# A hybrid attention and scan layer: the input projection taken in pairs of column slabs by a seven-product scheme, transposed, and kept in DRAM until attention and scan read it

## The chip, the cores and the metric

One core of a Trainium2 chip runs the whole layer. The metric is device time in microseconds (us); three runs of the kernel before gave a median of 1931.54 (1930.09 to 1934.35). The engines are named as the profile names them: PE (TensorE, matmul), PEld (its weight loads), DVE (VectorE), ACT (ScalarE), POOL (GpSimd), SP (SyncE, which here only issues DMAs).

## The reference

A sequence of 1024 tokens of width 1024 passes one layer:

```python
h = rmsnorm(x, g_pre)
q, k, v, g_att, z, xbc, dt, merge = split(h @ w_in)   # 1024 -> 12320 columns
o = diff_attention(q, k, v, rel_bias, lam)            # 8 heads, two softmax maps of width 64 each
y_att = (rmsnorm(o) * (1 - lambda_init) * silu(g_att)) @ w_att
xs, B, C = split(silu(causal_conv4(xbc)))             # 2048 + 8*128 + 8*128 columns
y = ssd_scan(xs, softplus(dt + dt_bias), -exp(a_log), B, C) + xs * d_skip
y_ssm = group_rmsnorm(y * silu(z)) @ w_ssm            # 8 groups
mixed = sigmoid(gate_att) * y_att + sigmoid(gate_ssm) * y_ssm
out = x + rmsnorm(mixed @ w_out, g_post)
```

All is float32. The projection `h @ w_in` is the largest product. In columns of 128 ("slabs") it has 8 each for q, k, v, g, 16 for z, 16 for x, 8 each for B and C, 16 for the gates, and 32 columns for dt.

## The kernel before

**Precision.** A float32 operand is kept as two tiles, a high half h (ACT copies the operand to a shorter format) and a low half l (the operand less h). `split` (L96) makes both: ACT the copy (L98), DVE or, if it is named, POOL the subtraction (L99). A product is three matmuls, h by h, h by l, l by h (`mm3`, L144; the matmul is L150). A slab of 128 columns for all tokens is thus 8 blocks of depth x 3 matmuls x 2 halves of 512 tokens, 48 matmuls of 512 columns.

**The start.** x is loaded in eight tiles, normed, transposed on PE (`ptx`, L235) and kept as hTH and hTL (L237, L238) through the whole kernel.

**The projection** is taken where it is needed. `load_cols` (L129) loads a slab of weights in two pieces of 128x512 and splits them. `proj_T` (L153) gives 128 output columns by 512 tokens in PSUM, for q, k, B, C, x and the gates; `proj_N` (L165) gives 128 tokens by 256 columns, for v with g, and for z. What comes out in PSUM is used there: L269 to L277 make the halves of q and k, L288 to L292 those of v and the gate, `conv_silu` (L498) copies it to the tile u and runs the convolution of four taps in two halves of 512 (L513, L515), L536 and L537 turn z into silu(z) in the token-major tile sz.

**Attention.** `attention` (L253) works a head after another, each in eight query blocks, `attend` (L311): scores `s` on PE (L322, L323), bias and maximum on DVE (L328, L331), the exponentials `p` on ACT (L342), the difference of the two maps on DVE (L357), transposes `pta` and their halves ah, al (L360 to L363), the product with v (`po`, L366, L367). The outputs are normed per head, multiplied by the gate (L305), transposed and stored in o_d.

**Scan.** `ssm` (L529) has eight groups; in each, eight chunks of 128 tokens pass through `prepare` (transposes px, xe at L578, xdt at L579, v on POOL at L580, the decay matrix mt: a load on ACT's DMA queue, ACT at L586 and L587, DVE at L588) and `advance` (products pd, the state st on POOL at L604, outputs v and yo at L609 to L614). `finish` norms, transposes and stores y_d.

**The order.** The Tile scheduler lays the instructions of each engine in one fixed order, by the program's order, dependences and buffers; an engine doesn't pass an instruction that waits. Gates (`gates`, L388) are projected between the heads and stored in sig_d. After the eight heads `branch_att` (L399) does the product with w_att, then the scan with its projections, then the rest of the gates, and at last (L655) the products with w_ssm and w_out.

Of the kernel before, what the change touches and what calls it, by code (L numbers as in the profile page):

```python
# [17 lines left out]
P = 128  # L18
# [5 lines left out]
DK = 64  # L24
# [23 lines left out]
CI, CU, CM, CE = 0, 128, 256, 384  # L48
NCONST = CE + NEAR
# [25 lines left out]
def tile_hybrid_layer(ctx: ExitStack, tc: tile.TileContext, x, g_pre, w_in, lq1, lk1, lq2, lk2,  # L75
# [9 lines left out]
    wts = ctx.enter_context(tc.tile_pool(name="wts", bufs=2))  # L85
# [33 lines left out]
    hTH = const.tile([P, KT, S], F32R, tag="hTH", name="hTH")  # L119
    hTL = const.tile([P, KT, S], F32R, tag="hTL", name="hTL")  # L120
# [6 lines left out]
    near_d = dram.tile([HEADS, NEAR], F32, name="near_d")  # L127

    def load_cols(w, row0, col0, width, tag, name, off=0, wh=None, wl=None, eng=None):  # L129

        if wh is None:
            wh = wts.tile([P, KT, width], F32R, tag=tag + "h", name=name + "h")
            wl = wts.tile([P, KT, width], F32R, tag=tag + "l", name=name + "l")
        for c in range(0, width - off, P):
            n = min(P, width - off - c)
            cols = slice(off + c, off + c + n)
            for k0 in range(0, KT, 4):
                raw = wts.tile([P, 4, P], F32, tag="raw", bufs=3, name=f"{name}r{off + c}_{k0}")
                r0 = row0 + k0 * P
                nc.sync.dma_start(raw[:, :, 0:n], w[r0:r0 + 4 * P, col0 + c:col0 + c + n].rearrange("(k p) c -> p k c", p=P))  # L140
                split(wh[:, k0:k0 + 4, cols], wl[:, k0:k0 + 4, cols], raw[:, :, 0:n], eng)
        return wh, wl

    def mm3(ps, terms):  # L144

        n = 3 * len(terms)
        i = 0
        for (ah, al), (bh, bl) in terms:
            for a, b in ((ah, bh), (ah, bl), (al, bh)):
                nc.tensor.matmul(ps, a, b, start=(i == 0), stop=(i == n - 1))  # L150
                i += 1

    def proj_T(w, half, name, rhs=None):  # L153

        wh, wl = w
        ps = psp.tile([P, 512], F32, tag="pp", name=name)
        sl = slice(half * 512, half * 512 + 512)
        if rhs is None:
            rhs = [(hTH[:, k, sl], hTL[:, k, sl]) for k in range(KT)]
        else:  # L160
            rhs = [(h[:, sl], l[:, sl]) for h, l in rhs]
        mm3(ps, [((wh[:, k, :], wl[:, k, :]), rhs[k]) for k in range(KT)])
        return ps

    def proj_N(w, t, n, name):  # L165

        wh, wl = w
        ps = psp.tile([P, 512], F32, tag="pp", name=name)
        sl = slice(t * P, (t + 1) * P)
        mm3(ps[:, 0:n], [((hTH[:, k, sl], hTL[:, k, sl]), (wh[:, k, 0:n], wl[:, k, 0:n])) for k in range(KT)])  # L170
        return ps
# [27 lines left out]
    with tc.tile_pool(name="norm", bufs=2, reuse_waits="tile") as work:  # L199
        def load_x(half):  # L200
            tiles = []
            for t in range(half * 4, half * 4 + 4):
                xt = work.tile([P, D], F32, tag="xt", bufs=8, name=f"xt{t}")
                nc.sync.dma_start(xt, x[t * P:(t + 1) * P, :])
                tiles.append(xt)
            return tiles

# [6 lines left out]
        nc.vector.tensor_copy(gcol, pg[:, 0:KT + 1])  # L214
        for half in range(2):
# [10 lines left out]
            for k in range(KT):  # L226
                if k % 4 < 2:
                    pt = pst.tile([P, 512], F32, tag="t", name=f"ptx{half}_{k}")
                elif k % 2 == 0:
# [183 lines left out]
    with tc.tile_pool(name="attn", bufs=2, reuse_waits="tile") as work:  # L413
        for h in range(HEADS):
            attention(h)
            gates(h)
# [320 lines left out]
```

## Time and profile before

| | |
|---|---|
| median of 3 runs | 1931.54 us |
| the profiled execution's own time | 1931.15 us |
| its span | 1929.4 us |
| granted TensorE clock | 0.989 |
| PE busy | 1828.1 us (95%), 10249 matmuls |
| DVE busy | 1183.5 us (61%), 2782 instructions |
| ACT busy | 862.4 us (45%) |
| POOL busy | 136.3 us (7%), 154 instructions |
| DMA | 169.34 MB, mean 88 GB/s |
| matmuls with w_att | from 734.43 us to the first with z's weights at 821.53 us |
| first matmul with w_ssm | 1640.72 us |

How to read what follows. A busy time is the time that the profiler shows instructions on an engine. Matmuls overlap, so the length of one (0.39) isn't its price; the distance between the starts of two in a row is. In a line of groups, "xN | busy, mean ns | idle before, releaser" gives the count, the sum, the mean of one, and what ended the idle time ahead of them. In a timeline the first number is the start, the second the length, and the bracket at the end is the idle time before it and what ended it. In a windows line the columns are the stretch, its length, then busy time (and count) of PE, PEld, DVE, ACT and POOL, the granted clock, the DMA share and GB/s.

### The profile page before, as it was taken

Reading aid. Unit: us, or ns where it says so; the run is one execution under the profiler, and the core shown is the slowest. Engines: PE = TensorE matmul, PEld = TensorE weight load, DVE = VectorE, ACT = ScalarE, POOL = GpSimd, SP = SyncE. Lnnn points to the kernel's source line nnn. Section 1 sums busy time; section 2 is a strip of 40 time slices with the busy share of each in tenths; the row PEclk is TensorE's granted clock in tenths of the full one; section 3 lists DMA queues with packets and bytes.
Section 4 is the critical chain, followed back from the end, with each engine's and each line's share of the span. In section 5 each row is a group of like instructions: output and inputs, shape, how many; then the busy total and the mean of one; then the engine's idle time right before and its main releaser. Section 6 shows DMA issues by size and latency. Waiting matters only on the chain. (4 is left out here: it accounts for less than half of the span.)

```text
span 1929.4 us, 27946 instructions
## 1 busy us (share of the span) xinstructions
PE 1828.1 (95%) x10249; PEld 1564.5 (81%) x10249; DVE 1183.5 (61%) x2782; ACT 862.4 (45%) x2135; POOL 136.3 (7%) x154
## 2 busy tenths in 40 slices
PE   6999999999999999999899989998989999999998
PEld 4888889789888878888787878787878777877786
DVE  5576486766757553247576767676757676545433
ACT  6455364545636442125445444545444545332221
POOL 1000000000000010001010101010101022000000
PEclk9999999999999999999999999999999999999999
DMA  6121222222122135513222222222222225653532
GB/s 204 55 75 56 53 58 59 70 61 60 54 54 66 37 125 178 166 34 79 70 61 72 63 69 63 70 65 71 63 64 64 69 50 173 220 172 134 175 110 71
DMA packets 222279, 169.34 MB, mean 88 GB/s; under 512 B 12733, under 2 KB 187167, under 8 KB 222143
## 3 DMA queue, kind: packets, MB, share of 16 engines
q1 hardware_dynamic: 169390, 117.21, 20.7%
q10 hardware_dynamic: 52752, 50.36, 9.0%
q8 instruction: 81, 1.33, 0.3%
q14 instruction: 56, 0.45, 0.1%
HBM read 129.63 MB, written 31.08 MB: 83 GB/s over the span
## 5 line engine op out<-in xcount | busy, mean ns | idle before, releaser
L150 PE MATMUL pz<-wzh,hTL 128*128 128x256 f32 (+1 forms) x512 | 152.0, 297 | 0.0
L150 PE MATMUL pz<-wzh,hTH 128*128 128x256 f32 (+1 forms) x512 | 149.6, 292 | 0.3 <-DVE dtr L539 0.3
L150 PE MATMUL pz<-wzl,hTH 128*128 128x256 f32 (+1 forms) x512 | 148.0, 289 | 0.0
L150 PE MATMUL pv<-wvh,hTH 128*128 128x256 f32 x512 | 144.5, 282 | 0.7 <-DVE kl L277 0.4
L150 PE MATMUL pv<-wvl,hTH 128*128 128x256 f32 x512 | 144.8, 283 | 0.0
L150 PE MATMUL pv<-wvh,hTL 128*128 128x256 f32 x512 | 144.0, 281 | 0.0
L586 ACT ACTIVATE mt<-mt,acs 128x128 f32<-128x128 f32 x256 | 85.6, 391 | 112.9 <-DMA mt<-arow_d 112.9
L580 POOL TENSOR_TENSOR v<-xb,dsk 128x256 f32<-128x256 f32 x64 | 51.1, 808 | 683.6 <-ACT xb L572 613.6
L331 DVE TENSOR_REDUCE ng<-s 128x2 f32<-128x1024 f32 (+2 forms) x96 | 91.3, 952 | 12.4 <-PE s L323 11.9
L150 PEld LDWEIGHTS pv<-wvh,hTH 128*128 128x128 f32 x512 | 97.0, 190 | 2.3 <-PE pv L150 0.5
L150 PEld LDWEIGHTS pz<-wzh,hTH 128*128 128x128 f32 x512 | 97.7, 191 | 1.5 <-PE pz L150 0.5
L150 PEld LDWEIGHTS pz<-wzl,hTH 128*128 128x128 f32 x512 | 97.6, 191 | 0.5
L150 PEld LDWEIGHTS pz<-wzh,hTL 128*128 128x128 f32 x512 | 97.1, 190 | 0.7
L150 PEld LDWEIGHTS pv<-wvl,hTH 128*128 128x128 f32 x512 | 96.7, 189 | 0.3
L150 PEld LDWEIGHTS pv<-wvh,hTL 128*128 128x128 f32 x512 | 96.2, 188 | 0.0
L342 ACT ACTIVATE p<-s,ngm 128x512 f32<-128x512 f32 (+3 forms) x128 | 76.7, 610 | 34.9 <-DVE ngm L337 34.8
L513 DVE SCALAR_TENSOR_TENSOR xT<-ux,cw,xT 128x512 f32<-128x512 f32 x96 | 75.7, 789 | 20.2 <-ACT xT L511 18.8
L607 PE MATMUL pd<-xdt,mt 128*128 128x64 f32 x512 | 66.6, 273 | 11.0 <-DVE st L605 4.8
L607 PEld LDWEIGHTS pd<-xdt,mt 128*128 128x128 f32 x512 | 62.4, 191 | 16.4 <-ACT mt L586 9.0
L366 PE MATMUL po<-vv,ah 128*128 128x256 f32 x288 | 74.8, 289 | 0.0
L289 DVE TENSOR_TENSOR vv<-pv,vv 128x128 fp32r<-128x128 f32 x64 | 18.6, 291 | 87.8 <-ACT vv L288 87.6
L367 PE MATMUL po<-vv,al 128*128 128x256 f32 x288 | 71.8, 282 | 0.0
(869 smaller groups left out, 5423.0 us busy)
## 6 DMA issues: line engine op xcount, KB each, us to landing
mt<-arow_d ACTq DMA_DIRECT2D x64, 256.0 KB, 4.9
sig_d<-gt ACTq DMA_DIRECT2D x32, 256.0 KB, 2.1
y_d<-yT ACTq DMA_DIRECT2D x32, 256.0 KB, 2.1
yT_l<-y_d SPq DMA_DIRECT2D x32, 256.0 KB, 5.7
xt<-in_x SPq DMA_DIRECT2D x8, 512.0 KB, 5.8
kh<-kh ACTq DMA_DIRECT2D x32, 128.0 KB, 2.3
kl<-kl ACTq DMA_DIRECT2D x32, 128.0 KB, 2.3
o_d<-oT ACTq DMA_DIRECT2D x16, 256.0 KB, 2.0
```

Of the source, the lines that this page charges most:

```text
L150: nc.tensor.matmul(ps, a, b, start=(i == 0), stop=(i == n - 1))
L289: nc.vector.tensor_tensor(vv[:, t, DV:], ps[:, 0:DV], f32(vv[:, t, 0:DV]), op=ALU.subtract)
L331: nc.vector.tensor_reduce(ng, s[:, :, 0:width], axis=AX.X, op=ALU.max, negate=True)
L342: nc.scalar.activation(p[:, m, lo:lo + width], s[:, m, 0:width], AF.Exp, bias=neg[:, m:m + 1], accum_out=sums[:, i, m:m + 1])
L366: nc.tensor.matmul(po[:, 0:256], ah[:, k, :], vv[:, k, :], start=(k == 0), stop=False)
L367: nc.tensor.matmul(po[:, 0:256], al[:, k, :], vv[:, k, :], start=False, stop=(k == qb))
L513: nc.vector.scalar_tensor_tensor(out_h, u[:, j:j + 512], cw[:, j, ct:ct + 1], out_h, op0=ALU.mult, op1=ALU.add)
L580: nc.gpsimd.tensor_tensor(v4(v), v4(xb[:, 0:256]), b4(dsk[:, hs]), op=ALU.mult)
L586: nc.scalar.activation(mt[:, i, :], mt[:, i, :], AF.Relu, scale=-1.0, bias=acs[:, c, g * HG + i:g * HG + i + 1])
L607: nc.tensor.matmul(pd[:, 0, i * PH:(i + 1) * PH], mt[:, i, :], xdt[:, i * PH:(i + 1) * PH], start=True, stop=True)
```

## The change

hTH, hTL, `load_cols`, `proj_T` and `proj_N` go from the projection. In their place stands `pair` (L160 of the changed kernel): two slabs of w_in at a time, all tokens, all transposed. Weights of a pair are seen as a 2 x 2 matrix of blocks (two slabs by two halves of the depth), h as a 2 x 2 matrix (two halves of the depth by two halves of the tokens), and the four blocks of the result come of seven products of blocks, where the plain way takes eight (Strassen's scheme in the form of Winograd). Each is 4 blocks of depth x 3 matmuls, so a pair takes 84 matmuls of 512 columns; two slabs took 96.

The seven combinations of h are made once, at the start (L249 and on), with the halves bh and bl; they take the room of hTH and hTL and more. The combinations of weights are made in each pair: s1 (L175), s2 (L176), a21 (L179) and s2 again (L195) by additions on POOL; each of seven operands is split by `halves` (L142), ACT for the high, POOL for the low half. The sums of the products go over four additions on DVE from PSUM (L189, L198, L208, L211), three copies on ACT, and one addition on POOL (L205). Gates go through ACT's tanh. Four stores on SP put a pair's halves into the DRAM tiles `slabs`.

What read PSUM before now loads a slab: q and k twice, so that the two maps lie as they did (`doubled`), v, which PE transposes (`ptv`), g, and in the scan u of the convolution at full width of 1024 and z, which PE transposes in `advance`. q's and k's low halves, the gate, the convolution and silu(z) thus work from SBUF on widths of 1024. The gate is kept transposed and multiplied into the transposed output (oT, on DVE). dt has its own small product (`steps`).

For the room that this takes, buffers shrink: x's tiles 8 to 6; qs and near 2 to 1; xT, bT, cT and sz 2 to 1; mt 3 to 2; v 7 to 6. The stores of o_d and y_d move from ACT's DMA queue to SP's. The pairs of head h+1 are written behind head h, the gates' pairs behind every second head and behind the first five scan groups, the pairs of scan group g+1 behind group g; `branch_att` moves behind the scan.

```diff
+    def halves(src, name):
+        h = prod.tile([P, 4, P], F32R, tag="ph", bufs=4, name=name + "h")
+        l = prod.tile([P, 4, P], F32R, tag="pl", bufs=4, name=name + "l")
+        split(h, l, src, nc.gpsimd)
+        return h, l
+
+    def product(ps, a, b, first):
+
         i = 0
...
+        for k in range(4):
+            for u, v in ((a[0], bh), (a[0], bl), (a[1], bh)):
+                nc.tensor.matmul(ps, u[:, k, :], v[:, b, k, :], start=first and i == 0, stop=i == 11,
+                                 skip_group_check=not first)
                 i += 1
...
+    def pair(c0, c1, gate=False):
...
+        a11, a21 = raw_half(c0, 0, f"a11_{nm}"), raw_half(c1, 0, f"a21_{nm}")
+        a22, a12 = raw_half(c1, 1, f"a22_{nm}"), raw_half(c0, 1, f"a12_{nm}")
...
+        p11 = halves(a11, f"p11_{nm}")
+        nc.gpsimd.tensor_tensor(s1, a21, a22, op=ALU.add)
+        nc.gpsimd.tensor_tensor(s2, s1, a11, op=ALU.subtract)
+        ps2 = halves(s2, f"ps2_{nm}")
+        p12 = halves(a12, f"p12_{nm}")
+        nc.gpsimd.tensor_tensor(a21, a21, a11, op=ALU.subtract)
+        ps3 = halves(a21, f"ps3_{nm}")
...
+        product(u, p11, B11, True)
+        m1 = staged(f"m1_{nm}")
+        nc.scalar.activation(m1, u, AF.Copy)
+        product(xx, ps2, T2, True)
+        x6 = staged(f"x6_{nm}")
+        nc.vector.tensor_tensor(x6, xx, m1, op=ALU.add)
+        ps1 = halves(s1, f"ps1_{nm}")
+        product(u, p12, B21, False)
+        c11 = staged(f"c11_{nm}")
+        nc.scalar.activation(c11, u, AF.Tanh if gate else AF.Copy, scale=0.5 if gate else 1.0)
+        nc.sync.dma_start(d0[:, 0:512], c11)
+        nc.gpsimd.tensor_tensor(s2, a12, s2, op=ALU.subtract)
+        product(xx, ps3, T3, False)
+        u3 = staged(f"u3_{nm}")
+        nc.vector.tensor_tensor(u3, xx, m1, op=ALU.add)
+        p22 = halves(a22, f"p22_{nm}")
...
+        product(v, ps1, T1, True)
+        m5 = staged(f"m5_{nm}")
+        nc.scalar.activation(m5, v, AF.Copy)
+        ps4 = halves(s2, f"ps4_{nm}")
+        nc.gpsimd.tensor_tensor(u3, u3, m5, op=ALU.add)
+        store(u3, d1, 1)
+        product(xx, p22, T4, False)
+        nc.vector.tensor_tensor(m1, xx, m1, op=ALU.add)
+        store(m1, d1, 0)
+        product(v, ps4, B22, False)
+        nc.vector.tensor_tensor(x6, v, x6, op=ALU.add)
+        store(x6, d0, 1)
...
-                xt = work.tile([P, D], F32, tag="xt", bufs=8, name=f"xt{t}")
+                xt = work.tile([P, D], F32, tag="xt", bufs=6, name=f"xt{t}")
...
+        def put(i, k, src, eng):
+            nc.scalar.activation(bh[:, i, k, :], src, AF.Copy)
+            eng.tensor_tensor(bl[:, i, k, :], src, f32(bh[:, i, k, :]), op=ALU.subtract)
...
+                    put(T2, k, t2, nc.vector)
+                    put(T3, k, t3, nc.gpsimd)
+                    put(T1, k, t1, nc.gpsimd)
+                    nc.gpsimd.tensor_tensor(t2, b1f[:, 4 + k, :], t2, op=ALU.subtract)
+                    put(T4, k, t2, nc.vector)
+                    put(B22, k, b22, nc.gpsimd)
...
+            q = doubled(OQ + h * P, half)
+            nc.scalar.activation(qs[:, :, sl], q, AF.Copy, scale=DK ** -0.5)
+            nc.vector.scalar_tensor_tensor(qs[hi, :, sl], q[hi], DK ** -0.5, f32(qs[hi, :, sl]), op0=ALU.mult, op1=ALU.subtract)
+            k = doubled(OK + h * P, half)
+            split(kh[:, :, sl], kl[:, :, sl], k)
...
+    def conv_silu(col, ct, dst, name):
+
+        u = work.tile([P, CONV - 1 + S], F32, tag="u", name=f"u{name}")
+        nc.gpsimd.memset(u[:, 0:CONV - 1], 0.0)
+        nc.sync.dma_start(u[:, CONV - 1:], slabs[col])
+        nc.scalar.activation(dst, u[:, CONV - 1:], AF.Identity, scale=cw[:, CONV - 1, ct:ct + 1], bias=cb[:, ct:ct + 1])
+        for j in range(CONV - 1):
+            nc.vector.scalar_tensor_tensor(dst, u[:, j:j + S], cw[:, j, ct:ct + 1], dst, op0=ALU.mult, op1=ALU.add)
+        nc.scalar.activation(u[:, 0:S], dst, AF.Tanh)
+        nc.vector.scalar_tensor_tensor(dst, u[:, 0:S], 1.0, dst, op0=ALU.add, op1=ALU.mult)
...
-            mt = work.tile([P, HG, P], F32, tag="mt", bufs=3, name=f"mt{nm}")
+            mt = work.tile([P, HG, P], F32, tag="mt", name=f"mt{nm}")
...
         for g in range(SG):
             ssm(g)
+            if g + 1 < SG:
+                for cols in ssm_pairs(g + 1):
+                    pair(*cols)
+            if g < 5:
+                pair(*gate_pairs[3 + g], gate=True)
```

Where the instructions come to stand is shown at three places, before and after. The first is POOL among the heads of attention. Before, POOL has two splits there in the time of one head (wm2, wm3, wm4 are the gates' weights behind three heads in a row):

```order
L99 TENSOR_TENSOR wm2l<-wm2r_0_3020,wm2h 128x512
L99 TENSOR_TENSOR wm2l<-wm2r_4_3024,wm2h 128x512
L99 TENSOR_TENSOR wm3l<-wm3r_0_3947,wm3h 128x512
L99 TENSOR_TENSOR wm3l<-wm3r_4_3951,wm3h 128x512
L99 TENSOR_TENSOR wm4l<-wm4r_0_4874,wm4h 128x512
L99 TENSOR_TENSOR wm4l<-wm4r_4_4878,wm4h 128x512
```

After, it has the splits and additions of whole pairs; 256_1280 is the pair of q's slab at column 256 and k's at 1280, for the third head:

```order
L175 TENSOR_TENSOR s_256_1280_1992<-a_256_1280_1986,a_256_1280_1988 128x512
L176 TENSOR_TENSOR s_256_1280_1993<-s_256_1280_1992,a_256_1280_1984 128x512
L179 TENSOR_TENSOR a_256_1280_1986<-a_256_1280_1986,a_256_1280_1984 128x512
L100 TENSOR_TENSOR p_256_1280l<-a_256_1280_1984,p_256_1280h 128x512
L100 TENSOR_TENSOR ps_256_1280l<-s_256_1280_1993,ps_256_1280h 128x512
L205 TENSOR_TENSOR u_2176_3200_1416<-u_2176_3200_1416,m_2176_3200_1435 128x512
L195 TENSOR_TENSOR s_256_1280_1993<-a_256_1280_1990,s_256_1280_1993 128x512
L100 TENSOR_TENSOR p_256_1280l<-a_256_1280_1990,p_256_1280h 128x512
L100 TENSOR_TENSOR ps_256_1280l<-a_256_1280_1986,ps_256_1280h 128x512
L100 TENSOR_TENSOR ps_256_1280l<-s_256_1280_1992,ps_256_1280h 128x512
L100 TENSOR_TENSOR p_256_1280l<-a_256_1280_1988,p_256_1280h 128x512
```

The weights' low halves have moved from DVE to POOL, with the additions of the scheme behind and between them; in all POOL has 749 rows, where it had 159.

The second place is PE in the attention of the second head, at the fourth query block's scores. Before, what stands between the steps of attention is the gate's projection pg, with hTH and hTL as the weights' partners:

```order
L322 MATMUL s_3_0_1743<-kh_1231,qs_1230 128x512
L323 MATMUL s_3_0_1743<-kl_1232,qs_1230 128x512
L150 MATMUL pg_0_2101<-hTH,wm1h 128x512
L150 MATMUL pg_0_2101<-hTL,wm1h 128x512
L366 MATMUL po_1_1696<-vv_1233,ah_1_1688 128x256
L150 MATMUL pg_0_2101<-hTH,wm1l 128x512
L367 MATMUL po_1_1696<-vv_1233,al_1_1689 128x256
```

After, the products of the next head's pair stand there, pu and px being two of the pair's sums in PSUM, and p_256_1280l the low half that POOL makes:

```order
L383 MATMUL s_3_0_1622<-kh_1472,qs_1471 128x512
L384 MATMUL s_3_0_1622<-kl_1473,qs_1471 128x512
L153 MATMUL pu_1280_2013<-bl,p_256_1280h 128x512
L153 MATMUL pu_1280_2013<-bh,p_256_1280l 128x512
L153 MATMUL pu_1280_2013<-bh,p_256_1280h 128x512
L153 MATMUL pu_1280_2013<-bl,p_256_1280h 128x512
L422 MATMUL pta_0_0_1539<-cst,p_0_0_1528 128x128
L153 MATMUL pu_1280_2013<-bh,p_256_1280l 128x512
L153 MATMUL pu_1280_2013<-bh,p_256_1280h 128x512
L427 MATMUL po_0_1543<-vv_1474,ah_0_0_1536 128x256
```

What fills PE between the attention's own steps is now a product of a pair, and each such filler stands ahead of the attention's next step.

The third place is DVE in the convolution of the scan's x. Before, four operations of width 512 per half, with weights' splits of the group's other slabs (wb1) between them:

```order
L513 SCALAR_TENSOR_TENSOR xT_8909<-ux_0_9103,cw,xT_8909 128x512 x3
L515 SCALAR_TENSOR_TENSOR xT_8909<-ux_0_9103,xT_8909 128x512
L513 SCALAR_TENSOR_TENSOR xT_8909<-ux_1_9137,cw,xT_8909 128x512 x2
L99 TENSOR_TENSOR wb1l<-wb1r_0_9850,wb1h 128x512
L513 SCALAR_TENSOR_TENSOR xT_8909<-ux_1_9137,cw,xT_8909 128x512
L99 TENSOR_TENSOR wb1l<-wb1r_4_9854,wb1h 128x512
L515 SCALAR_TENSOR_TENSOR xT_8909<-ux_1_9137,xT_8909 128x512
```

After, operations of width 1024, with the pairs' additions from PSUM between them (L208 and L211 of one pair, L189 of the next):

```order
L559 SCALAR_TENSOR_TENSOR xT_8922<-ux_8944,cw,xT_8922 128x1024
L208 TENSOR_TENSOR m_4352_4480_8668<-px_4480_8655,m_4352_4480_8668 128x512
L559 SCALAR_TENSOR_TENSOR xT_8922<-ux_8944,cw,xT_8922 128x1024
L211 TENSOR_TENSOR x_4352_4480_8682<-pv_4480_8722,x_4352_4480_8682 128x512
L559 SCALAR_TENSOR_TENSOR xT_8922<-ux_8944,cw,xT_8922 128x1024
L559 SCALAR_TENSOR_TENSOR xT_8922<-ux_8953,cw,xT_8922 128x1024
L561 SCALAR_TENSOR_TENSOR xT_8922<-ux_8944,xT_8922 128x1024
L559 SCALAR_TENSOR_TENSOR xT_8922<-ux_8953,cw,xT_8922 128x1024
L189 TENSOR_TENSOR x_11040_11168_8830<-px_11168_8803,m_11040_11168_8816 128x512
```

The convolution now stands behind the scan of the group before it, whose tiles it writes over, and PE's next product of a pair stands behind the addition that frees its PSUM tile.

More of the change, by code (lines that the diff above doesn't have):

```diff
@@ L151, in mm3, with staged @@
                 i += 1
[L153 to L171, printed above, removed]
+    def staged(name):
+        return prod.tile([P, 512], F32, tag="st", bufs=6, name=name)
@@ L399, in branch_att @@
[L399 to L411 removed]
+    dt_d = dram.tile([SH, S], F32, name="dt_d")
```

389 lines of the change are left out of this document (199 added, 190 removed).

## The prediction, made before the changed kernel had run

> **What bounds the kernel now.** First the page: busy time of each engine.
>
> ```profile
> PE 1828.1 (95%) x10249; PEld 1564.5 (81%) x10249; DVE 1183.5 (61%) x2782; ACT 862.4 (45%) x2135; POOL 136.3 (7%) x154
> ```
>
> TensorE (PE) is busy 95% of the span, VectorE (DVE) 61%, ScalarE (ACT) 45%, GpSimd (POOL) is all but free. Then the windows of one attention head (its dense half, its loose half) and of one scan group (its steps, its convolutions):
>
> ```profile
> 160.00:195.00 35.00, 35.00 (x189) 29.15 (x188) 29.61 (x74) 23.18 (x71) 0.00 (x0) 1.00 0.24 68
> 195.00:244.00 49.00, 46.43 (x314) 41.99 (x314) 24.00 (x60) 17.41 (x47) 2.61 (x2) 0.97 0.20 52
> 1374.00:1422.00 48.00, 43.37 (x321) 40.81 (x319) 34.66 (x92) 23.20 (x64) 10.63 (x14) 0.96 0.22 56
> 1422.00:1470.00 48.00, 45.88 (x203) 37.18 (x202) 30.59 (x66) 23.76 (x47) 0.00 (x0) 0.96 0.28 76
> ```
>
> The columns after the length are PE, weight loads, DVE, ACT, POOL. A head takes 84 us, a group 96, and PE works 81.4 and 89.3 of them: PE sets the pace. But in the dense half DVE already works 29.6 of 35. So the kernel is PE-bound with a second engine close behind in two places. PE's price, from the timelines, is the distance of starts:
>
> ```profile
> 1559.41 0.40 PE L150 MATMUL pux<-hTH,wx17l 128*128 128x512 f32 x1
> ...
> 1569.21 0.40 PE L150 MATMUL pux<-hTH,wx17l 128*128 128x512 f32 x1
> 53.97 0.28 PE L150 MATMUL pv<-wvh,hTH 128*128 128x256 f32 x1
> ...
> 55.14 0.28 PE L150 MATMUL pv<-wvl,hTH 128*128 128x256 f32 x1
> 103.17 0.27 PE L360 MATMUL pta<-cst,p 128*128 128x128 f32 x1
> 103.28 0.27 PE L306 MATMUL pto<-cst,o 128*128 128x128 f32 x1
> ```
>
> 42 steps of 512 columns take 9.80 us, 0.233 each; 256 columns 0.117; a transpose 0.11.
>
> **What PE saves.** Two slabs cost 84 matmuls of 512 columns in place of 96 (or of their equal in halves of 256). 48 pairs: 576 x 0.233 = 134 us less. New on PE are 64 transposes of v and 128 of sz, with a few others 200 x 0.11 = 22 us, and dt 48 matmuls by itself, 8 us more than inside the z projection. Net 104 us, 5% of the time. That is all that can be won.
>
> **What POOL gets.** A pair has 12 POOL instructions of 128x512 (7 low halves, 5 additions), 576 in all. The page has such an instruction, and the scan's own:
>
> ```profile
> L99 POOL TENSOR_TENSOR wm5l<-wm5r,wm5h 128x512 fp32r<-128x512 f32 x2 | 2.5, 1294 | 81.5 <-ACT wm5h L98 81.5
> L580 POOL TENSOR_TENSOR v<-xb,dsk 128x256 f32<-128x256 f32 x64 | 51.1, 808 | 683.6 <-ACT xb L572 613.6 <-DVE sz L537 70.0
> ```
>
> At 1.28 a pair costs POOL 15.4 us against 19.6 of PE (84 x 0.233): alone it would keep up. 576 x 1.28 = 737 us, the norm's 16 x 1.28 = 20, and the scan's own (136.3 of the page less the 38 splits that POOL has now, 49) 87: about 845 us, where it had 136. DVE in turn gives up its 154 splits of weights, 106 us at the 0.69 that mt, of the same shape, takes below. The question is who else stands still meanwhile. The timelines of DVE and POOL in the one place where both work on SBUF side by side:
>
> ```profile
> 209.57 0.16 DVE L108 SCALAR_TENSOR_TENSOR rst_o<-rst_o,rsv_o 128x4 f32<-128x4 f32 x1
> 209.76 1.15 DVE L109 SCALAR_TENSOR_TENSOR rsy_o<-rst_o,rsy_o 128x4 f32<-128x4 f32 x1
> 210.94 0.16 DVE L107 TENSOR_TENSOR rst_o<-rsy_o 128x4 f32<-128x4 f32 x1
> 211.34 1.25 DVE L109 SCALAR_TENSOR_TENSOR rsy_o<-rst_o,rsy_o 128x4 f32<-128x4 f32 x1
> 209.58 1.31 POOL L99 TENSOR_TENSOR wm2l<-wm2r,wm2h 128x512 fp32r<-128x512 f32 x1 [77.55 <-DVE rst_o L107]
> 211.27 1.30 POOL L99 TENSOR_TENSOR wm2l<-wm2r,wm2h 128x512 fp32r<-128x512 f32 x1 [0.38 <-ACT wm2h L98]
> 1383.02 0.68 DVE L588 TENSOR_TENSOR mt<-mt,cbm 128x512 f32<-128x512 f32 x1
> 1383.62 0.83 DVE L578 TENSOR_TENSOR xe<-xb,dend 128x256 f32<-128x256 f32 x1
> 1383.17 0.99 POOL L604 TENSOR_TENSOR st<-st,elast 128x256 f32<-128x256 f32 x1 [0.89 <-DVE st L602]
> 1387.03 0.61 POOL L604 TENSOR_TENSOR st<-st,elast 128x256 f32<-128x256 f32 x1
> 129.43 0.69 DVE L272 SCALAR_TENSOR_TENSOR qs<-pq,qs 64x512 fp32r<-64x512 f32 x1
> 129.49 2.54 POOL L99 TENSOR_TENSOR wm1l<-wm1r,wm1h 128x512 fp32r<-128x512 f32 x2 [77.22 <-ACT wm1h L98]
> ```
>
> A four-element DVE operation, 0.16 us otherwise, lasts 1.15 and ends (210.91) as POOL's ends (210.89); the next pair does it again. In the scan POOL's st (0.61 a few us on) starts beside mt and takes 0.99, and DVE's xe, which began meanwhile, ends behind it. So a DVE operation with two operands in SBUF and a POOL operation run one behind the other. Line 272, with one operand in PSUM, kept its 0.69 beside POOL.
>
> The Trainium skill ("SBUF — State Buffer", section "Who interferes with whom") says it so: the port pair that DVE shares with GpSimd is an exclusive lock, an instruction of two SBUF inputs takes it, and whoever issues second blocks fully. The trace agrees (1.15 us for 0.16); by that rule the change's POOL work is also DVE waiting, which speaks against it.
>
> How much of DVE is of that kind: its groups by line.
>
> ```profile
> L513 DVE SCALAR_TENSOR_TENSOR xT<-ux,cw,xT 128x512 f32<-128x512 f32 x96 | 75.7, 789 | 20.2 <-ACT xT L511 18.8
> L357 DVE SCALAR_TENSOR_TENSOR p<-p,nlam 128x512 f32<-128x512 f32 (+2 forms) x96 | 59.1, 634 | 0.7
> L588 DVE TENSOR_TENSOR mt<-mt,cbm 128x512 f32<-128x512 f32 x64 | 44.0, 688 | 24.5 <-ACT mt L587 24.4
> L579 DVE TENSOR_TENSOR xdt<-xb,dts 128x256 f32<-128x256 f32 x64 | 35.7, 557 | 0.0
> L578 DVE TENSOR_TENSOR xe<-xb,dend 128x256 f32<-128x256 f32 x56 | 32.9, 588 | 3.8 <-ACT xb L572 3.7
> L613 DVE TENSOR_TENSOR v<-v,yo 128x256 f32<-128x256 f32 x56 | 24.0, 428 | 0.1
> L515 DVE SCALAR_TENSOR_TENSOR xT<-ux,xT 128x512 f32<-128x512 f32 x32 | 22.1, 690 | 17.6 <-ACT ux L514 17.6
> L99 DVE TENSOR_TENSOR oTl<-oTl,oTh 128x1024 fp32r<-128x1024 f32 x8 | 10.2, 1286 | 11.7 <-ACT oTh L98 11.6
> ```
>
> The convolution of all slabs is twice 75.7 and twice 22.1 (B and C have as many rows as x): 196. With p, mt, xdt, xe and v: 392. The change turns q, k, g and z, until now read from PSUM, into 1024-wide operations on SBUF: five per head and two per group, 56 x 1.29 = 72 us. With small ones, as in the timeline, I take 500 to 560. So 845 + 530 = 1375 us must pass one behind the other before the scan's end, in a stretch that may last 1550 for the old time to stand (1931 less the tail's 289, w_att's 70 and 20 of loading, all below): nearly nine tenths of perfect packing, for two engines with fixed orders and short buffers (four ph and pl).
>
> **Stage by stage.** Counts come from the order of the changed kernel, durations from the rows, DVE's stretches from the mean of each form in before.
>
> Start. Before, transposes begin at 13.54, the second half's at 31.46, and q and k are done at 53.97. With these, the first scores, the start of the tail, and two prices used below (mt's load, an ACT split):
>
> ```profile
> 13.54 3.70 PE L235 MATMUL ptx<-cst,xt 128*128 128x128 f32 x16 [4.01 <-DVE xt L225]
> 31.46 0.63 PE L235 MATMUL ptx<-cst,xt 128*128 128x128 f32 x4 [1.82 <-DVE xt L225]
> 60.34 0.28 PE L323 MATMUL s<-kl,qs 128*128 128x256 f32 x1
> 1640.72 0.39 PE L150 MATMUL pys<-yT_h,wp_0h 128*128 128x512 f32 x1
> mt<-arow_d ACTq DMA_DIRECT2D x64, 256.0 KB, 4.9
> L98 ACT ACTIVATE yT_h<-yT_l 128x512 fp32r<-128x512 f32 x32 | 19.1, 626 | 8.3 <-DMA yT_l<-y_d 6.2 <-PE pys L150 1.5 <-ACT gt L396 0.4
> ```
>
> Now six buffers of x hold two tiles of the second half back (37 in place of 31), and 16 POOL operations (20.5) and 12 of DVE on SBUF (8.3) follow one another before the first products that need the seven combinations: first pair at 79. The second pair, then v's load and transposes: 20. First scores at about 99; before they ran at 60.34.
>
> Dense halves, first scores of a head to its last: PE 40 (94 fill matmuls among them), DVE 43 of its own (the window's 29.6, four additions per pair from PSUM at 0.69, and the scaling and gate of the output and the 1024-wide operations that now fall here). About 13 POOL operations lie in the stretch; each that meets a p, q, k or gate operation holds it half its length, 0.64, on average, and nearly all meet one: 13 x 0.64 = 8. So 51, eight times 408. DVE becomes the bound, and PE waits: its order puts a fill between two heads' steps, so that a low half that is late stops the scores behind it, for which DVE's reduction then waits. Loose halves: PE 25 in four, 43 in three that hold a gate pair, DVE 15 to 21; 229. Last head to the first scan: conv in the open, POOL 54 + DVE 35 under the lock, PE 75: 85.
>
> Scan groups 1 to 4: the steps have PE 42, DVE 41, POOL 13 pair operations and its own eight and six (28 us), half of DVE's under the lock: 58. The rest of the group: 35 POOL operations (45) and convolution, sz and small ones on DVE (26.5) make 71.5 against PE's 57, and the convolution can't start sooner, since its tiles have one buffer now: 75. So 133, four times 532. Group 0 105, 5 and 6, with fewer pairs, 120 each, 7 (only w_att to fill) 75. What is left of w_att: 301 x 0.233 = 70. The tail, from 1640.7 to 1929.4 now, is untouched: 289.
>
> 79 + 20 + 408 + 229 + 85 + 532 + 105 + 240 + 75 + 70 + 289 = 2132, and 1.75 for what lies around the span (1931.15 of the profiled execution less 1929.4): about 2130. That execution lies 0.4 under the median 1931.54, so no correction. ACT's part (7 splits and 3 evictions of some 0.63, 6.3 us a pair, under PE's 19.6), and SyncE's queue, which now takes slab stores, reloads and the stores of o and y in between the weight loads, I cost at nothing: the windows' DMA share of 0.20 to 0.28 leaves room, and PE or the lock covers what a store holds back (the raw loads behind it have six buffers). Uncovered, one late load costs about the 4.9 us of mt's.
>
> **Rivals.**
> A, faster: PE stays the bound and the lock costs nothing, because blocked DVE operations have slack. For it: DVE idles 39%. Against: 1.15 for 0.16 wherever they met. Start 71 + 20, dense 8 x 41 = 328, loose 228, first scan 76, groups 1 to 4 at 99 and 5 and 6 at 80 over the 0.93 that PE reaches in a group (89.25 of 96) 426 + 172, groups 0 and 7 105 + 75, 70, 289: 1860. Chance 0.16.
> B, slower, but milder: POOL works ahead by its buffers and the convolutions slip between; rest of a group 61 in place of 75 (57 / 0.93), groups 5 and 6 100, group 0 100: 2132 - 56 - 40 - 5 = 2030. Chance 0.25.
> C, slower still: two mt buffers in place of three. A step of the scan then lasts at least half of load (4.9) and the work of ACT, DVE and PE on it (I take as long again): 4.9 us against 7.3 of my 58 / 8, so hidden; it decides once POOL holds the chain up by over 5 us a step. At 9.5 a step, 8 x 18 more: 2275. Chance 0.07.
> That the change doesn't do what it says is out: its order has the 84 matmuls per pair.
>
> **The numbers.** My forecast, 2130, has 0.49 (2055 to 2205, by 5 us either way on the eight dense halves and 6 on groups 1 to 6), no change 0.03: it would take a lock that costs a quarter of what I count, 70 of the 270 us between A and the forecast. The range 1950 to 2260 leaves out A, and C's end. Measured differences under about 0.2% mean no change here. Faster is A, 0.16; slower are B, C and the forecast, 0.81.
>
> **What would show it.** Right: PE's busy share near 80%; POOL about 845 us; DVE operations on two SBUF operands (p, mt, xe, convolution) longer by tenths of a us, PSUM ones not; the idle of PE before fills put down to POOL's low halves and DVE's additions; first scores near 99; groups near 130. Wrong: p and mt keep 0.63 and 0.69 beside a POOL at 40%; PE at 90% or more (A); or ACT's queue and mt's loads end PE's waits in the scan (C).

## The result, and the profile after

The changed kernel takes 2118.94 us (median of 4 runs, 2115.36 to 2122.18) against 1932.94 before: a ratio of 1.0957, 95% interval 1.0921 to 1.0992. The forecast was 2130 in a range from 1950 to 2260. The sum came out within 11 us; its terms did not come out as well, as the table of stages below shows.

The page of the changed kernel, its busy times, and three rows of 40 slices:

```profile
PE 1797.3 (85%) x8385; PEld 1440.0 (68%) x8385; DVE 1398.6 (66%) x2463; ACT 954.3 (45%) x2114; POOL 974.2 (46%) x744
...
PE   4888898888889877888888888888888869898998
...
POOL 4835454454453446656675867667484510000000
PEclk7889999999999999989999999999999989999999
```

PE has 1864 matmuls fewer and is not the bound any more: 85% in place of 95%. POOL is busy 974 us, where 845 were counted, and DVE 1399 us with 319 instructions fewer than before. Both are longer than their work, and the groups of DVE say which part:

```profile
L559 DVE SCALAR_TENSOR_TENSOR xT<-ux,cw,xT 128x1024 f32<-128x1024 f32 x48 | 86.9, 1830 | 47.5 <-ACT xT L557 47.3
L419 DVE SCALAR_TENSOR_TENSOR p<-p,nlam 128x512 f32<-128x512 f32 (+2 forms) x96 | 91.9, 970 | 0.6
L100 DVE TENSOR_TENSOR al<-pta,ah 128x512 fp32r<-128x512 f32 (+2 forms) x96 | 51.6, 551 | 22.6 <-ACT ah L99 21.7
L613 DVE TENSOR_TENSOR mt<-mt,cbm 128x512 f32<-128x512 f32 x64 | 50.4, 788 | 16.4 <-ACT mt L612 16.4
L603 DVE TENSOR_TENSOR xe<-xb,dend 128x256 f32<-128x256 f32 x56 | 40.5, 723 | 14.1 <-ACT xb L597 13.8
L636 DVE TENSOR_TENSOR v<-pd,v 128x256 f32<-128x256 f32 x64 | 26.5, 416 | 8.0 <-PE pd L635 7.2
```

Before, al and v were:

```profile
L363 DVE TENSOR_TENSOR al<-pta,ah 128x512 fp32r<-128x512 f32 (+2 forms) x96 | 51.8, 553 | 14.3 <-ACT ah L362 13.8
L609 DVE TENSOR_TENSOR v<-pd,v 128x256 f32<-128x256 f32 x64 | 27.0, 421 | 10.5 <-PE pd L607 10.2
```

The mean of one is the number to compare: p 970 ns (634 before), mt 788 (688), xe 723 (588). These read two operands in SBUF. al and v, which read one in PSUM, kept theirs: 551 (553) and 416 (421). POOL's own additions got longer too, 1.28 us having been counted for each:

```profile
L179 POOL TENSOR_TENSOR a<-a,a 128x512 f32<-128x512 f32 x48 | 79.4, 1654 | 3.3
```

How that looks from inside: the timelines of DVE and of POOL in the convolution that follows the steps of the fourth scan group.

```profile
1318.77 2.31 DVE L561 SCALAR_TENSOR_TENSOR xT<-ux,xT 128x1024 f32<-128x1024 f32 x1
1321.01 2.30 DVE L559 SCALAR_TENSOR_TENSOR xT<-ux,cw,xT 128x1024 f32<-128x1024 f32 x1
1323.23 0.68 DVE L208 TENSOR_TENSOR m<-px,m 128x512 f32<-128x512 f32 x1
1324.50 2.30 DVE L561 SCALAR_TENSOR_TENSOR xT<-ux,xT 128x1024 f32<-128x1024 f32 x1 [0.59 <-ACT ux L560]
1326.72 0.68 DVE L211 TENSOR_TENSOR x<-pv,x 128x512 f32<-128x512 f32 x1
```

```profile
1317.84 2.15 POOL L176 TENSOR_TENSOR s<-s,a 128x512 f32<-128x512 f32 x1
1319.96 2.26 POOL L100 TENSOR_TENSOR p_11936l<-a,p_11936h 128x512 fp32r<-128x512 f32 x1
1322.18 2.27 POOL L100 TENSOR_TENSOR ps_11936l<-s,ps_11936h 128x512 fp32r<-128x512 f32 x1
1324.42 1.29 POOL L205 TENSOR_TENSOR u<-u,m 128x512 f32<-128x512 f32 x1
1325.67 2.26 POOL L195 TENSOR_TENSOR s<-a,s 128x512 f32<-128x512 f32 x1
1327.88 1.31 POOL L100 TENSOR_TENSOR p_11936l<-a,p_11936h 128x512 fp32r<-128x512 f32 x1
```

The two engines take turns. A convolution step starts at 1321.01 while POOL works until 1322.22, runs then, and ends at 1323.31; POOL's next one, begun at 1322.18, waits for that and ends at 1324.45. Each shows 2.3 us for 1.3 us of work. POOL's operation at 1324.42, begun while DVE was idle, takes 1.29, and the convolution step that follows waits for it; the one at 1327.88 meets no step of two operands in SBUF and takes 1.31. L208 and L211, which read PSUM, keep 0.68 beside POOL.

The windows of the second head (first scores to last, last scores to the next head's first) and of the fourth scan group (steps, rest), with PE, PEld, DVE, ACT, POOL in the columns and the granted clock behind them:

```profile
189.60:236.70 47.10, 44.38 (x233) 35.69 (x232) 40.26 (x84) 28.22 (x83) 19.22 (x15) 1.00 0.33 101
236.70:284.20 47.50, 41.12 (x202) 33.81 (x200) 29.76 (x48) 22.02 (x43) 29.00 (x22) 0.96 0.45 136
1226.00:1267.00 41.00, 35.76 (x208) 28.65 (x209) 35.09 (x82) 21.75 (x59) 21.83 (x23) 1.00 0.34 90
1267.00:1353.00 86.00, 71.65 (x294) 56.17 (x292) 51.03 (x54) 36.98 (x63) 64.60 (x45) 0.92 0.43 132
```

The steps of a group take 41 us, as they did before the change (898.47 to 939.53 in the first group). What grew is the rest: 86 us, POOL busy in 64.6 of them. What PE waited for there:

```profile
PE px L153 <- DVE x L189: 4.4, 1, 4.4
PE px L153 <- DVE u L198: 4.2, 1, 4.2
PE pty L654 <- DVE v L650: 2.4, 1, 2.4
```

L189 and L198 are additions from PSUM, which POOL doesn't delay. But each stands in DVE's queue behind a step that needs a slab from DRAM: L189 behind the first convolution step of xT, L198 behind silu(z). How the first of these waits came about, on SP's queue, ACT, DVE and PE:

```profile
1302.81 0.37 SPq L556 DMA_DIRECT2D ux<-pj  x1
1307.34 1.24 ACT L557 ACTIVATE xT<-ux,cg,cw 128x1024 f32<-128x1024 f32 x1 [6.40 <-DMA ux<-pj]
1308.66 1.28 DVE L559 SCALAR_TENSOR_TENSOR xT<-ux,cw,xT 128x1024 f32<-128x1024 f32 x1 [8.23 <-ACT xT L557]
1309.87 0.68 DVE L189 TENSOR_TENSOR x<-px,m 128x512 f32<-128x512 f32 x1
1310.61 0.80 PE L153 MATMUL px<-bh,ps_5248h 128*128 128x512 f32 x1 [4.38 <-DVE x L189]
```

DVE stands idle for 8.23 us until ACT has the slab, and then its step takes 1.28, no longer than undisturbed. So this wait isn't time that POOL took from DVE: the slab came late. Its load left SP behind a load of weights, for which SP's queue had waited 2.6 us on POOL; POOL's lengthened operations thus have a part in it, which no run here separates. Before L198, DVE is idle 9.16 us in the same way. Over the groups there are nine such waits of PE, of 4.0 to 4.4 us, 38 us together.

By stage, in us, from the starts of the first scores, last scores, first pd and first product with w_ssm in the timelines of PE. The last column is an experiment told below, in which POOL is as busy but reads next to nothing, and the scheduler's order differs in part:

| stage | before | forecast | after | POOL without reading |
|---|---|---|---|---|
| start to first scores | 57 | 99 | 103 | 94 |
| the eight heads, of it dense / loose | 632 | 408 / 229 | 386 / 274 | 349 / 225 |
| last scores to first pd (before: with w_att) | 209 | 85 | 111 | 95 |
| first pd to first product with w_ssm (scan, gates; after: with w_att) | 742 | 1022 | 960 | 870 |
| tail | 289 | 289 | 286 | 286 |
| sum | 1929 | 2132 | 2120 | 1919 |

### The profile page after: what moved, and what is told of

The parts are those of the page before. It is cut to its first block, busy times and chain, and to the rows that moved or that the text cites. A ratio compares the mean times of both kernels' runs of the same rounds, so it can differ in the third digit from the quotient of the medians.

```text
span 2119.5 us, 25585 instructions
## 1 busy us (share of the span) xinstructions
PE 1797.3 (85%) x8385; PEld 1440.0 (68%) x8385; DVE 1398.6 (66%) x2463; ACT 954.3 (45%) x2114; POOL 974.2 (46%) x744
## 5 line engine op out<-in xcount | busy, mean ns | idle before, releaser
L559 DVE SCALAR_TENSOR_TENSOR xT<-ux,cw,xT 128x1024 f32<-128x1024 f32 x48 | 86.9, 1830 | 47.5 <-ACT xT L557 47.3
L175 POOL TENSOR_TENSOR s<-a,a 128x512 f32<-128x512 f32 x48 | 78.0, 1625 | 31.3 <-DMA a<-in_w_in 28.4
L419 DVE SCALAR_TENSOR_TENSOR p<-p,nlam 128x512 f32<-128x512 f32 (+2 forms) x96 | 91.9, 970 | 0.6
L205 POOL TENSOR_TENSOR u<-u,m 128x512 f32<-128x512 f32 x48 | 70.5, 1468 | 26.9 <-ACT m L203 26.9
L179 POOL TENSOR_TENSOR a<-a,a 128x512 f32<-128x512 f32 x48 | 79.4, 1654 | 3.3
L176 POOL TENSOR_TENSOR s<-s,a 128x512 f32<-128x512 f32 x48 | 76.0, 1583 | 3.3
L195 POOL TENSOR_TENSOR s<-a,s 128x512 f32<-128x512 f32 x48 | 74.7, 1556 | 1.0
L383 PE MATMUL s<-kh,qs 128*128 128x512 f32 (+2 forms) x192 | 72.4, 386 | 0.9 <-ACT p L403 0.9
L422 PE MATMUL pta<-cst,p 128*128 128x128 f32 x288 | 51.7, 287 | 24.9 <-DVE p L419 22.1
L384 PE MATMUL s<-kl,qs 128*128 128x512 f32 (+2 forms) x192 | 68.8, 368 | 0.0
L208 DVE TENSOR_TENSOR m<-px,m 128x512 f32<-128x512 f32 x48 | 32.9, 685 | 48.7 <-PE px L153 48.2
```

What stands on the lines that cost most here:

```text
L175: nc.gpsimd.tensor_tensor(s1, a21, a22, op=ALU.add)
L176: nc.gpsimd.tensor_tensor(s2, s1, a11, op=ALU.subtract)
L179: nc.gpsimd.tensor_tensor(a21, a21, a11, op=ALU.subtract)
L419: nc.vector.scalar_tensor_tensor(pi[:, 0], pi[:, 1], nlam, pi[:, 0], op0=ALU.mult, op1=ALU.add)
L422: nc.tensor.transpose(pt[:, j * P:(j + 1) * P], pi[:, 0, j * P:(j + 1) * P], ident)
L559: nc.vector.scalar_tensor_tensor(dst, u[:, j:j + S], cw[:, j, ct:ct + 1], dst, op0=ALU.mult, op1=ALU.add)
```

## The experiments

The theory: a POOL operation and a DVE operation with two operands in SBUF exclude each other, and the time lost is what that costs. Rivals: POOL is a slow link in each pair's own chain, whatever DVE does; the way through DRAM with single buffers sets the length of a group; the third mt buffer is missed.

**Low halves on DVE.**

```diff
-        split(h, l, src, nc.gpsimd)
+        split(h, l, src)
```

> The seven low halves of a pair go from POOL to DVE, the five additions stay on POOL. Lock theory (a POOL operation and a DVE operation with two SBUF operands exclude each other, and the sum of both is what fills the stages): 336 operations of 1.28 us turn into as many of 0.69, the sum under the lock falls by about 198 us, and with some of that hidden the time falls from 2119 to 1990 to 2050; means of POOL's additions fall from about 1.6 towards 1.3. Rival, the chain (POOL as one link in each pair is slow by itself, and its own time counts, not the exclusion): also faster, by what POOL's 64 us in a group's loose part exceed PE's 57, some 7 to 15 us a group and as much a head, 1950 to 2010. Rival, the spill (the trip of the slabs through DRAM, with single buffers behind the scan, sets the length of a group): 2100 to 2130, no change.

Measured 1994.16 us, ratio to before 1.0321 [1.0284, 1.0358]: within the lock's range, and within the chain's too. The spill as the main cause is out. One thing that was expected did not come: the means of POOL's additions stayed at 1.45 to 1.64 us in place of falling towards 1.3.

**The five additions on DVE instead**, low halves on POOL; all five calls of `pair` as this one:

```diff
-        nc.gpsimd.tensor_tensor(s1, a21, a22, op=ALU.add)
+        nc.vector.tensor_tensor(s1, a21, a22, op=ALU.add)
```

> The complement of the first experiment: the five additions of a pair go to DVE, the seven low halves stay on POOL. If what counts is only how many operations lie under the lock, each of the 336 moved there was worth 125 / 336 = 0.37 us, and 240 moved give 89: 2030. If the two parts make up the whole gain of 232 between them, 2119 - 107 = 2012. If the additions count more because the splits wait for them (a chain within the pair): under 1990.

Measured 2051.59, 1.0641 [1.0608, 1.0674]: 67 us less than the changed kernel, a smaller gain than any expectation had. 0.28 us per operation moved in place of 0.37, so the additions are worth less, not more, than the splits; a chain that hangs on them is not seen. That the two parts together (125 + 67) give less than both at once (232) is what an exclusion would do that bites until POOL is nearly empty, but the run doesn't show why. The scheduler's order of the instructions changes with each of these edits, and no run holds it fixed.

**All twelve on DVE**, both edits together.

```diff
-        split(h, l, src, nc.gpsimd)
+        split(h, l, src)
...
-        nc.gpsimd.tensor_tensor(s1, a21, a22, op=ALU.add)
+        nc.vector.tensor_tensor(s1, a21, a22, op=ALU.add)
```

> All twelve POOL operations of a pair go to DVE; POOL keeps the scan's and the start's. Lock theory: nothing is left to exclude in the pairs, DVE's two-operand operations fall back to their length alone (p 0.63, convolution 1.5, mt 0.69), but DVE takes 576 x 0.69 = 397 us more, about 1600 in all, and becomes the bound in the dense halves: 1960 to 2020. Chain: POOL's slowness gone, 1900 to 1950. Spill: 2090 to 2130.

Measured 1887.08, 0.9778 [0.9751, 0.9805]: faster than before the change by 2.2%, and below every range that was expected: the lock theory's (1960 to 2020, with DVE as the bound) and the chain's (1900 to 1950). Its page:

```profile
PE 1729.1 (92%) x8385; PEld 1403.0 (74%) x8385; DVE 1478.9 (79%) x3042; ACT 949.9 (50%) x2114; POOL 118.7 (6%) x165
```

DVE took over the pairs' 576 operations, and its busy time rose by only 80 us. In the next run, which has these operations nowhere, DVE is busy 1156.0 us; so they add 323 (less than 576 x 0.69 = 397, since operations in a row overlap a little, as in the timeline above), and some 243 of the changed kernel's 1398.6 were waiting that the profile books as work.

**No POOL work in the pairs at all.**

```diff
-        split(h, l, src, nc.gpsimd)
+        nc.scalar.activation(h, src, AF.Copy)
...
-        nc.gpsimd.tensor_tensor(s1, a21, a22, op=ALU.add)
-        nc.gpsimd.tensor_tensor(s2, s1, a11, op=ALU.subtract)
```

> The pairs without any POOL work and without putting it elsewhere: the combinations of weights and the low halves of weights are left out (a tile of zeros stands for the low halves, the slabs' own halves for the combinations, the last addition is not done), while every matmul, ACT copy, DVE addition from PSUM and DMA stays. It shows what all of POOL's work in the pairs costs. Lock theory and chain: PE is the bound again, 1840 to 1900, granted clock back at 0.98. Spill: over 2000.

Measured 1852.73, 0.9593 [0.9561, 0.9626], 78 us under the kernel before: with the POOL work gone, most of PE's saving arrives. It is within 7 us of rival A's sum, 1860, though A has POOL at work and only its cost at nothing. Its page:

```profile
PE 1716.6 (93%) x8385; PEld 1393.9 (75%) x8385; DVE 1156.0 (62%) x2464; ACT 950.2 (51%) x2114; POOL 112.6 (6%) x165
```

**The kernel before with idle POOL additions.**

```diff
+    def extra(t, n=23):
+        nc.gpsimd.tensor_tensor(idle[:, 0:P], t, ident, op=ALU.add)
+        for _ in range(n):
+            nc.gpsimd.tensor_tensor(idle, cst, cst, op=ALU.add)
...
+        extra(gg[:, 7, :])
...
+                extra(o_t[0])
...
+        extra(vs[6][:, 0:P], 40)
```

> The kernel before, with 712 POOL additions added that read a constant tile twice and write a tile that nobody reads (128x384, about 0.97 us each; 47 in each head from its attention on, 41 in each group's convolutions): no engine waits for their result, so only the exclusion can cost time. Lock theory: p, the convolution and the splits of weights on DVE get longer by tenths of a us beside them, operations that read PSUM don't; DVE, with 29.6 of 35 us in the dense half, has to wait there, so a head gets 4 to 8 us longer, a group 0 to 6: 1970 to 2040. Chain theory: 1930, unchanged, means unchanged.

Measured 2081.22, 1.0768 [1.0732, 1.0804]: 148 us, more than was expected, for work that no engine waits for. The page's busy times, then the group of p and that of al:

```profile
PE 1875.3 (90%) x10249; PEld 1581.1 (76%) x10249; DVE 1372.9 (66%) x2782; ACT 862.2 (41%) x2135; POOL 798.9 (38%) x866
```

```profile
L366 DVE SCALAR_TENSOR_TENSOR p<-p,nlam 128x512 f32<-128x512 f32 (+2 forms) x96 | 80.3, 853 | 0.7
L372 DVE TENSOR_TENSOR al<-pta,ah 128x512 fp32r<-128x512 f32 (+2 forms) x96 | 52.0, 552 | 8.0 <-ACT ah L371 7.2
```

The same 2782 DVE instructions take 189 us longer; p goes from 634 to 853, al stays. A chain of the pairs has no part in this kernel, and neither has the scheduler's order: by the traces PE and ACT run their instructions in the same order as in the kernel before, DVE all but 8 of them.

**The same with memsets.**

```diff
-            nc.gpsimd.tensor_tensor(idle, cst, cst, op=ALU.add)
+            nc.gpsimd.memset(idle, 0.0)
```

> The same with a memset of the same width in place of each addition but the first of a run: POOL is busy at the same places but reads nothing. Lock theory, if it is the reading that excludes: 1930 to 1940, DVE's means as before. If any POOL operation excludes DVE: as the additions, in proportion to POOL's busy time. Chain theory: 1930.

Measured 1946.0, 1.007 [1.0043, 1.0096], with the order of the kernel before on PE, ACT and DVE. p is back:

```profile
L366 DVE SCALAR_TENSOR_TENSOR p<-p,nlam 128x512 f32<-128x512 f32 (+2 forms) x96 | 59.3, 636 | 0.7
```

POOL is busy 438 us in this kernel (421 ns for a memset, 947 for an addition), so it is not the same dose; in proportion to POOL's added time (302 against 663 us) the additions' 148 would be 67. It is 13, of which 24 additions of 128 columns that are left may have a part. These two runs show the cause: with the order kept, a POOL that reads costs 148 us, and one that writes, at a little under half the dose, 13.

**POOL as busy, but reading next to nothing**, in the changed kernel.

```diff
+    def held(o, a, b):
+        n = (slice(None), 0, slice(0, 8)) if len(o.shape) == 3 else (slice(None), slice(0, 8))
+        nc.gpsimd.tensor_tensor(o[n], a[n], b[n], op=ALU.subtract)
+        for _ in range(2):
+            nc.gpsimd.memset(o if o.dtype == F32 else f32(o), 0.0)
...
-        split(h, l, src, nc.gpsimd)
+        nc.scalar.activation(h, src, AF.Copy)
+        held(l, src, f32(h))
```

> The changed kernel with every POOL operation of the pairs kept as a link at its place, waiting for the same operands and waited for by the same readers, but done as an 8-column operation and two memsets of 128x512 that write zeros (low halves and combinations of weights are thus left out): POOL is busy in the pairs for about as long (2 x 0.55 and a small one, against 1.28), reads almost nothing. Lock theory: what the exclusion costs is gone, p and the convolution are back at 0.63 and 1.3, near the kernel without POOL work (1853): 1855 to 1930. Chain theory (POOL as a slow link, with its queue and the four buffers): 2050 to 2119.

Measured 1914.04, 0.9898 [0.987, 0.9926], in the lock's range. The page, p and the convolution, and the windows of the same head's two halves and the same group's two parts:

```profile
PE 1738.9 (91%) x8385; PEld 1408.2 (73%) x8385; DVE 1176.4 (61%) x2463; ACT 949.0 (49%) x2114; POOL 844.7 (44%) x1902
```

```profile
L426 DVE SCALAR_TENSOR_TENSOR p<-p,nlam 128x512 f32<-128x512 f32 (+2 forms) x96 | 57.2, 611 | 0.5
L566 DVE SCALAR_TENSOR_TENSOR xT<-ux,cw,xT 128x1024 f32<-128x1024 f32 x48 | 60.1, 1280 | 24.7 <-ACT xT L564 21.6 <-POOL a L146 2.8
```

```profile
162.30:209.40 47.10, 46.07 (x244) 37.66 (x243) 39.14 (x93) 29.96 (x85) 20.75 (x51) 1.00 0.39 120
209.40:248.60 39.20, 38.38 (x195) 31.37 (x193) 22.65 (x48) 21.10 (x42) 23.35 (x57) 1.00 0.53 158
1072.20:1110.20 38.00, 34.93 (x204) 27.89 (x205) 30.70 (x79) 21.69 (x59) 19.43 (x39) 1.00 0.33 97
1110.20:1185.90 75.70, 69.49 (x298) 55.73 (x297) 37.47 (x55) 36.66 (x63) 53.09 (x125) 0.95 0.48 146
```

POOL is busy 844.7 us, as long as the 845 that the prediction counted for its work without waiting, and the same 2463 DVE instructions take 222 us less than in the changed kernel. In ratios to before: 1.0957 with the reading, 0.9898 without it, 0.9593 without POOL. The first step is 0.106 of 1933, 205 us; the second, POOL's own time and its place in the chains, 0.031, 59 us.

The 205 us are not the exclusion alone. The scheduler laid this kernel's instructions in an order of its own: all of them are there, but in the heads nearly half of DVE's stand elsewhere in its queue, and in the scan, where the order is else nearly the same, L189 (L196 here) stands ahead of the convolution step for whose slab it waited:

```profile
1145.17 0.69 DVE L196 TENSOR_TENSOR x<-px,m 128x512 f32<-128x512 f32 x1 [4.80 <-PE px L160]
1150.30 5.00 DVE L566 SCALAR_TENSOR_TENSOR xT<-ux,cw,xT 128x1024 f32<-128x1024 f32 x4 [4.44 <-ACT xT L564]
```

PE's waits for L189 and L198 together are 63.6 us in the changed kernel and 7.2 here. How the 205 us divide between the reading and the order, no run shows. That the reading costs what it does to DVE's own instructions is shown by their 222 us, and that it costs time with the order kept by the two runs on the kernel before.

**Three mt buffers**, and, for the room, five staging tiles in place of six.

```diff
-            mt = work.tile([P, HG, P], F32, tag="mt", name=f"mt{nm}")
+            mt = work.tile([P, HG, P], F32, tag="mt", bufs=3, name=f"mt{nm}")
```

> The changed kernel with three buffers for the decay matrix mt, as before the change (the pairs' staging tiles go from six to five for the room). Lock theory: 2105 to 2120, nothing to gain, since the scan's steps of a group take 41 us as they did before. Rival C of the prediction (two mt buffers hold up the steps): 2060 or less.

Measured 2131.9, 1.1048 [1.1014, 1.1083]: no gain, rather 0.6% lost by the medians (0.8% by the ratios), which may be the staging tile or the order. Rival C is out: a step of the scan, moreover, lasts 41 / 8 = 5.1 us, not the 9.5 that C needs.

**Plain products, the spill alone.**

```diff
+                product(ps, a, i, True)
+                product(ps, b, j, False)
+                t = staged(f"c_{nm}_{half}")
+                nc.scalar.activation(t, ps, AF.Tanh if gate else AF.Copy, scale=0.5 if gate else 1.0)
```

> The transposed projection through DRAM alone, with plain products: four blocks of weights per pair split on DVE, eight products (96 matmuls), no combinations of weights or of h, four copies on ACT; POOL has nothing but the scan's. It tells the scheme of seven products from the spill. 576 matmuls more than the kernel with all on DVE are 134 us, the DVE work that goes (8 operations a pair, 0.69 each) gives back up to 35, the start 10 to 20: 1950 to 1990, so slower than before by 1 to 3%. If the spill by itself cost much more (its waits, not PE, set the length): over 2020.

Measured 1936.44, 1.0036 [1.002, 1.0052]: better than expected. The transposed way through DRAM costs next to nothing by itself in this kernel, which also has eight buffers for the weights' halves in place of four. Against all work on DVE (1887), the seven products gain 49 us of the 134 that their matmuls are worth; where the other 85 go, the runs don't separate. The operations that make the combinations are the likeliest place: the first scores come at 97 us there and at 81 here.

**The best version**: the edits of all twelve on DVE, the start's too, and three mt buffers, with five staging tiles (only the start's lines are shown).

```diff
-                    put(T3, k, t3, nc.gpsimd)
-                    put(T1, k, t1, nc.gpsimd)
-                    nc.gpsimd.tensor_tensor(t2, b1f[:, 4 + k, :], t2, op=ALU.subtract)
+                    put(T3, k, t3, nc.vector)
+                    put(T1, k, t1, nc.vector)
+                    nc.vector.tensor_tensor(t2, b1f[:, 4 + k, :], t2, op=ALU.subtract)
```

> All of the pairs' and the start's POOL work on DVE, mt with three buffers, five staging tiles: what the experiments point to as the best so far. Against the 1887 of all pair work on DVE: the start has 16 operations of 0.69 on DVE in place of 1.28 to 1.6 on POOL, 0 to 8 us; the third mt buffer 0 to 20. Expected 1865 to 1887, so 2 to 3% under the kernel before.

Measured 1885.49, 0.9771 [0.9747, 0.9794]: not told apart from the 1887 of the version with the pairs' work alone on DVE. Both beat both kernels, by 2.2 to 2.3% under the one before.

## Why the prediction was right, and which of its terms were not

**PE's saving** was right in kind. Net 104 us was argued; 78 arrive once the pairs have no POOL work.

**The exclusion** was right as a rule. In size it was taken too high: the forecast put all 270 us between itself and A down to it. By the runs the pairs' POOL work costs 264 us, 205 between reading and not reading, the changed order among them, and 59 for POOL being busy. These 59 the prediction had at nothing ("alone it would keep up"). Two POOL subtractions next to four-element operations in the trace of before were enough to see it. The Trainium skill's rule ("SBUF — State Buffer", section "Who interferes with whom") says besides that a GpSimd instruction that only writes doesn't take part; the two runs with memsets agree (p at 636 and 611 beside them).

**Where it bites** was wrong, and this is the step that failed: "half of DVE's under the lock: 58" for the steps of a group, and the dense halves as the place where DVE becomes the bound. (How 58 comes of DVE's 41 and POOL's 28 isn't shown; 41 and half of 28 are 55.) The steps took 41, 3 more than with a POOL that doesn't read (38). POOL had 21.8 us of work in them, against the 28 that were counted, and DVE 35 against 41. The dense halves took 386 in place of 408, 37 more than without reading, though not in every head: the second head's is 47.1 in both. The loose halves were taken at PE's time, 229, and took 274, where without reading they take 225. The rest of a group was put at 75 and took 86 (75.7 without reading).

The prediction had summed POOL's and DVE's lengths in one stage and compared the sum with PE. What it missed is the queues, in two places. In the loose halves PE's transposes wait for the head's norm, a chain of small steps on DVE, each 0.16 us and beside POOL up to 1.3. PE's waits for its result, over the whole span, in the changed kernel and without reading:

```profile
PE pto L366 <- DVE o L365: 44.4, 15, 4.5
PE pto L373 <- DVE o L372: 12.0, 9, 2.6
```

In the rest of a group the pairs' additions stand behind steps that wait for a slab, as shown above; that is SyncE's queue with its reloads, which the prediction also costed at nothing. Of the signs that it named, one did not come: PE's own waits name none of the pairs' low halves, only DVE and ACT in front of the pairs' products.

The errors have both signs (measured less forecast: groups -62, heads +23, the way to the first scan +26, start +4, tail -3) and leave -12 of 2132. So the sum was right in part by luck; that it would be slower, and by what means, was worked out from the right cause.

**The granted clock** was left out. It is 0.940 over the span after, 0.989 before, 0.964 without reading. PE's timeline behind a wait shows what it does:

```profile
1272.33 0.39 PE L153 MATMUL pu<-bl,p_7296h 128*128 128x512 f32 x1
1275.15 0.41 PE L654 MATMUL pty<-cst,v 128*128 128x128 f32 x2 [2.44 <-DVE v L650]
...
1277.90 0.63 PE L153 MATMUL pu<-bh,p_7296h 128*128 128x512 f32 x1
1278.32 0.63 PE L153 MATMUL pu<-bl,p_7296h 128*128 128x512 f32 x1
...
1279.50 0.39 PE L153 MATMUL px<-bl,ps_7296h 128*128 128x512 f32 x1
1279.73 0.39 PE L153 MATMUL px<-bh,ps_7296l 128*128 128x512 f32 x1
```

After 2.4 us without work the matmuls come 0.42 us apart for a few us, then 0.23 again. 6% of 2119.5 us are 127 us of clock, 21 before; part of it fell on time in which PE waited anyway, and no run here separates what is left. The start, at 0.78 to 0.79, is the longest such stretch.

**Rival B**, that POOL works ahead and the convolutions slip between, did not happen: it gave the rest of a group 61 us, and that took 86. It was the steps that hid the exclusion.

## What to carry to other kernels

Before work goes to GpSimd because it is idle, look at what VectorE does at that time: operations of two SBUF operands and GpSimd operations that read SBUF run one behind the other, so taking 0.69 us of work off VectorE can block it for up to the 1.28 us that the work takes on GpSimd. Here the same work on the busy engine was 232 us faster than on the idle one. A sum of both against the bound showed that there would be a loss and came near its size, in part by luck; where it falls is decided by who stands in the queue behind the blocked instruction. And an edit to one instruction can change the scheduler's order of all: before a difference is put down to the edit, compare the orders.

## What the runs showed of the hardware that was not expected

GpSimd additions that nobody waits for cost a kernel 148 us in 1933, with 663 us of them. Memsets of the same width took 421 ns where the additions took 947, and VectorE's two-operand operations kept their length beside them. A convolution step of 1024 columns takes 1.28 us undisturbed (the mean without reading), and 1.83 in the changed kernel.
